# A two-layer encoder trunk on one core: where three pieces of work stand in the written order, and how the input is cut

## The chip, the cores and the metric

The kernel runs on one core of one Trainium2 chip. The core has five engines: PE (TensorE, matrix products and transposes into the accumulation memory, PSUM), DVE (VectorE), ACT (ScalarE), POOL (GpSimd) and SP (SyncE, which here only issues DMAs). The metric is the device time of one launch in microseconds (us), as the median of several runs. A profile is one execution taken by the hardware profiler, and its span runs from the first instruction of the program to the last.

## The reference, cut to what matters

The input is `x`, 512 tokens by 1024 features in float32. Two layers follow one another.

```python
def swiglu_ffn(h, w_up, w_down):
    a, b = jnp.split(h @ w_up, 2, axis=-1)
    return (jax.nn.silu(a) * b) @ w_down

for l in range(DEPTH):                       # DEPTH = 2
    x = x + 0.5 * swiglu_ffn(rmsnorm(x, ffn1_norm[l]), ffn1_w_up[l], ffn1_w_down[l])
    x = x + mixer(rmsnorm(x, mix_norm[l]), ...)
    x = x + 0.5 * swiglu_ffn(rmsnorm(x, ffn2_norm[l]), ffn2_w_up[l], ffn2_w_down[l])
    x = rmsnorm(x, final_norm[l])
```

The mixer projects its input once (`w_in`). From the columns it computes dilated sliding-window attention in three groups of eight heads (dilations 1, 4, 16; scores, a mask, a softmax, a product with the values), a convolution of width 31 over the tokens with a layer norm and a projection, two gates, and a last projection (`w_out`).

## The kernel before

Activations lie transposed: eight tiles `xs[k]` of 128 features by 512 tokens. Every float32 product is made as three products of a high and a low part (`mm3`, L156 to L159: high by high, low by high, high by low), so each activation and each weight is kept as a pair `hi`, `lo`. A weight block is staged by `stage` (L140): one DMA of 512 KB into `raw`, a copy to `hi` on ACT (L152), a difference to `lo` on DVE (L153).

**The start** (L76 to L81, L714 to L731). Four DMAs load `xnat`, one for each 128 tokens, all 1024 features wide. For each feature block k, PE transposes a square of each of the four tiles into `ps_x` (L721). Then `gained` makes `xgh` on ACT (L174) and `xgl` on DVE (L175), with which the first feed-forward product starts. ACT also squares each `xnat` tile for the norm (L727).

**The feed-forward** `ffn` (L315). For a pair of hidden blocks m it computes the two halves of the up-projection, `ps_a` and `ps_b`, 16 groups of three matmuls of 128x512 each; then `t2` takes `ps_a` times the norm factor R (L340, DVE), a Silu (L341, ACT), the product with `ps_b` (L345, DVE) and a split (`hh`, `hl`). From m = 4 (`M7`) on, the second half goes through `proj7`, which saves products by a seven-product scheme (84 matmuls of 128x256). It needs sums of the activations: `sums7` (L265), for each of four pairs of feature blocks: two additions into `t2` (L324), then L269 to L271, and a split (`Th`, `Tl`). These sums are written ahead of the loop over m. `deferred` (L349) is, in the second layer's first feed-forward, the rescaling of `xs` by the last layer's final norm: eight DVE instructions (L780) that read `R1`. It is written behind m = 0. R and R1 reach all partitions by two products each on PE (`ps_bc`, L214), which end the preceding feed-forward.

**The attention** `attend` (L507). It is called for three groups and two halves of the heads. A unit is one block of 128 queries in group 0 (four units for a call) and two blocks in the others (two units). It computes scores into two PSUM tiles `ps_S` (L528), one for each parity e of the head. For each e in turn it then does: a mask with a row minimum on DVE into `sp` (L541), exponentials on ACT (L547), four transposes on PE into `ps_T` (L550), and a copy on ACT into `PT` (L552). Then come sixteen products with the values into `ps_pv` (L558). Around the units lie the projections of the next group (`ps_n`, evicted by L451 and L483, transposed by L473), and on DVE the 480 convolution taps (L620), written behind them all.

**What sets the order.** The order on each engine is fixed when the program is built. A planner plays the program through and gives each engine, whenever it is free, the ready instruction that is written earliest; the staging of weights and a few other parts are moved up. On the chip each engine then works its list strictly in that order. A tile name has a fixed number of buffers, which its tiles share: `t2` has 2 buffers for the sums and the hidden blocks together, `sp` and `PT` share 6, `raw` has 2, `hi` and `lo` have 4 each. Of the eight PSUM banks `ps_a` and `ps_n` use 3, all of `ps_b`, the four of `proj7`, `ps_x`, `ps_S`, `ps_T`, `ps_pv` and `ps_qT` share 4 (tag "at"), and `ps_bc` uses the one that is left. A new feed-forward takes its memory over from the one before it once all readers of that are done.

```python
t2 = fp.tile([P, 2, S], F32, tag="t2", name=uniq("g2"), bufs=2)    # L322, sums
t2 = fp.tile([P, 2, S], F32, tag="t2", name=uniq("t2"), bufs=2)    # L337, hidden block
sp = slot("sp", 6)                                                 # L531
t = slot("sp", 6, name="PT")                                       # L551
```

Of the kernel before, what the change touches and what calls it, by code (L numbers as in the profile page):

```python
# [11 lines left out]
F32 = mybir.dt.float32  # L12
F32R = mybir.dt.float32r
AF = mybir.ActivationFunctionType
ALU = mybir.AluOpType
# [4 lines left out]
P = 128  # L20
D = 1024
# [23 lines left out]
def trunk(ctx: ExitStack, tc: tile.TileContext, A: dict, out: bass.AP):  # L45
# [14 lines left out]
    def ps_at(name):  # L60
        return psp.tile([P, S], F32, tag="at", name=name, bufs=4)
# [11 lines left out]

    x0s = ExitStack()
    x0 = x0s.enter_context(tc.tile_pool(name="x0", bufs=1))
    xnat = []  # L76
# [59 lines left out]
    def uniq(s):  # L136
        cnt[0] += 1
        return f"{s}_{cnt[0]}"
# [176 lines left out]
    def ffn(l, w_up, w_down, xg, R, after, deferred=None):  # L315
        wu = w_up[l].rearrange("(k p) n -> p k n", p=P)
        wd = w_down[l].rearrange("(k p) n -> p k n", p=P)
        with tc.tile_pool(name=uniq("ffn"), bufs=4) as fp:
            few.add(id(fp))
            x7 = []  # L320
            for q in range(0, KD, 2):
                t2 = fp.tile([P, 2, S], F32, tag="t2", name=uniq("g2"), bufs=2)  # L322
                for j in range(2):
                    nc.vector.tensor_add(t2[:, j], xg[q + j][0].bitcast(F32), xg[q + j][1].bitcast(F32))  # L324
                x7.append(sums7(fp, t2, xg[q:q + 2], "T", 8))
            for m0, m1 in PARTS:
                h = []
                for m in range(m0, m1, 2):
                    pss = {}
                    for ab in ((0, 1) if m < M7 else (1, 0)):  # L330
                        if ab == 1 and m >= M7:
                            o = proj7(fp, wu, FF + m * P, x7, False)
                            pss[1] = [o[:, 0], o[:, 1]]
                            continue
                        pss[ab] = [ps_mm(uniq("ps_a")) if ab == 0 else ps_at(uniq("ps_b")) for _ in range(2)]
                        proj_cols(wu, ab * FF + m * P, xg, KD, pss[ab])
# [24 lines left out]
                for ts in ((0, 1), (2, 3), (4, 5), (6,), (7,)) if last else ((0, 1), (2, 3), (4, 5), (6, 7)):  # L361
                    pss = [(ps_at if ts[0] in (0, 4, 7) else ps_mm)(uniq("ps_d")) for _ in ts]
                    proj_cols(wm, ts[0] * P, h, m1 - m0, pss)
                    for k, ps in zip(ts, pss):
                        take(k, ps, 0.5)


    def mixer(l, xg, R, rr, after):
# [5 lines left out]
        with ExitStack() as mx:  # L374
            mp = mx.enter_context(tc.tile_pool(name=uniq("mix"), bufs=2))

            def slot(tag, bufs, dt=F32, name=None):
                return mp.tile([P, S], dt, tag=tag, name=uniq(name or tag), bufs=bufs)
# [128 lines left out]
            def attend(g, hh, qkT, V):  # L507
# [6 lines left out]
                for b2 in range(0, 4, 2):  # L514
                    po = ps_at(uniq("ps_pv"))
                    pv = po.rearrange("p (i b q) -> p i b q", i=2, b=2)
                    for bs in ([[b2], [b2 + 1]] if g == 0 else [[b2, b2 + 1]]):
                        lo, hi = 0, n
                        if g == 0:
                            lo, hi = (64 if bs[0] == 0 else 0), (192 if bs[0] == 3 else 256)  # L520

                        pS = [ps_at(uniq("ps_S")) for _ in range(2)]
                        work = [(b, i) for b in bs for i in range(2)]
                        for w, (b, i) in enumerate(work):
                            k0 = b * P - 64 if g == 0 else b * P
                            for e in range(2):
                                hp = slice(e * 64, e * 64 + 64)
                                nc.tensor.matmul(pS[e][:, w * n + lo:w * n + hi], qkT[hp, i, b * P:(b + 1) * P], qkT[hp, 2 + i, k0 + lo:k0 + hi], start=True, stop=True)  # L528
                        PT = []
                        for e in range(2):  # L530
                            sp = slot("sp", 6)  # L531
                            sv = sp.rearrange("p (w k) -> p w k", k=n)
                            if lo:
                                nc.vector.memset(sv[:, :, :lo], 0.0)
                            if hi < n:
                                nc.vector.memset(sv[:, :, hi:], 0.0)

                            for w, (b, i) in enumerate(work):
                                c = slice(w * n + lo, w * n + hi)
                                h = 2 * i + e  # L540
                                nc.vector.tensor_tensor_reduce(  # L541
                                    out=sp[:, c], in0=pS[e][:, c], in1=mask[:, lo:hi], scale=1.0, scalar=3e38,
                                    op0=ALU.add, op1=ALU.min, accum_out=st[:, b, h:h + 1])
                            for w, (b, i) in enumerate(work):
                                c = slice(w * n + lo, w * n + hi)
                                h = 2 * i + e
                                nc.scalar.activation(sp[:, c], sp[:, c], AF.Exp, bias=st[:, b, h:h + 1], scale=-1.0, accum_out=st[:, b, UH + h:UH + h + 1])  # L547
                            pT = ps_at(uniq("ps_T"))
                            for i in range(4):
                                nc.tensor.transpose(pT[:, i * P:(i + 1) * P], sp[:, i * P:(i + 1) * P], ident)  # L550
                            t = slot("sp", 6, name="PT")  # L551
                            nc.scalar.activation(t, pT, AF.Copy)  # L552
                            PT.append(t)
                        for w, (b, i) in enumerate(work):
                            for j in range(nj):
                                for e in range(2):
                                    h = 2 * i + e
                                    nc.tensor.matmul(pv[e * 64:(e + 1) * 64, i, b - b2, :], V[b + j][:, (hh * UH + h) * HD:(hh * UH + h + 1) * HD], PT[e][:, (nj * w + j) * P:(nj * w + j + 1) * P], start=j == 0, stop=j == nj - 1)  # L558
                    for i in range(2):
                        dst = ot[i].rearrange("p (a r) -> p r a", r=dil)  # L560
                        if g == 0:
                            dst = dst[:, :, b2 * P:(b2 + 2) * P]
                        else:
                            dst = dst[:, b2 * dil // 4:(b2 + 2) * dil // 4, :]
                        nc.scalar.activation(dst, po[:, i * 256:(i + 1) * 256].rearrange("p (r a) -> p r a", a=dst.shape[2]), AF.Copy)
                for i in range(2):
                    nc.gpsimd.dma_start(od[g, 2 * hh + i], ot[i])
                so = sd[:, g, hh, :]
# [289 lines left out]
```

## Time and profile before

| what | value |
|---|---|
| median of 3 runs | 2653.77 us (2652.79 to 2654.54) |
| profiled execution | 2655.37 us |
| its span | 2653.3 us |
| PE busy | 2593.0 us, 98% |
| PE weight loads busy | 2168.9 us, 82% |
| DVE busy | 1984.0 us, 75% |
| ACT busy | 1100.8 us, 41% |
| PE on the chain that ended last | 92% |
| mean DMA rate | 101 GB/s |

A line of the profile names an engine, the line of the kernel, the operation, the tile written and the tiles read. Where an engine was idle before an instruction, the page names what ended that idle time. PEclk is the share of TensorE's full clock (2.4 GHz) that was granted: 1.00 is full speed, 0.50 is 1.2 GHz. Since PE is busy for 98% of the span, the time can fall only by what PE spends idle and by what it spends at the lower clock.

### The profile page before, as it was taken

The page shows a single profiled execution, that of the slowest core. Times are in us where ns is not written, and L with a number is a line of the kernel's source. Part 1 is how long each engine was busy: PE and PEld are TensorE (multiplying, and loading weights), DVE is VectorE, ACT ScalarE, POOL GpSimd, SP SyncE. Part 2 cuts the span into 40 slices and gives each one's busy share as a digit, 9 for nine tenths or more (in the row PEclk, how much of TensorE's full clock was granted, in tenths as well). Part 3 has the DMA queues.
Part 4 walks back from the last instruction along what each step waited for, and adds up shares of the span by engine and source line. Part 5 has one row for each costly group of instructions (what it writes and reads, how often), then busy time and mean ns, then how long its engine had stood idle before and what let it go on. Part 6 is the DMA issues. An engine that isn't in the chain of part 4 may idle for free.

```text
span 2653.3 us, 34486 instructions
## 1 busy us (share of the span) xinstructions
PE 2593.0 (98%) x13421; PEld 2168.9 (82%) x13421; DVE 1984.0 (75%) x3218; ACT 1100.8 (41%) x1651; POOL 110.8 (4%) x208
## 2 busy tenths in 40 slices
PE   8999999998999999999979999999999999999998
PEld 6888988776877788888868989887767777888887
DVE  6666669999986667666766766699999866666665
ACT  5333342243587234233433333422445773433334
POOL 1000000011011000000000000000011110000000
PEclk9999999999999999999989999999999999999999
DMA  4323333232333333232313333332323343233322
GB/s 143 104 92 108 92 108 105 84 119 89 108 108 113 111 96 104 88 111 91 101 55 111 96 104 96 103 105 88 110 88 120 104 129 104 88 104 96 108 92 80
DMA packets 245603, 268.87 MB, mean 101 GB/s; under 512 B 11624, under 2 KB 230128, under 8 KB 245440
## 3 DMA queue, kind: packets, MB, share of 16 engines
q1 hardware_dynamic: 233920, 234.91, 28.5%
q0 software_dynamic: 11504, 31.76, 4.1%
q8 instruction: 105, 1.72, 0.3%
q14 instruction: 58, 0.48, 0.1%
q10 hardware_dynamic: 16, 0.00, 0.0%
HBM read 251.75 MB, written 14.88 MB: 100 GB/s over the span
## 4 chain that ended last, share of the span: by engine, by line
PE 92%; DVE 6%; ACT 1%; issue 1%; DMA 0%; SPq 0%; ACTq 0%
PE ps_a L158 6%; PE ps_a L159 6%; PE ps_a L157 6%; PE ps_d L158 6%; PE ps_d L157 6%; PE ps_d L159 6%; PE ps L159 5%; PE ps L158 5%; PE ps L157 5%; PE ps_n L158 4%; PE ps_n L157 4%; PE ps_n L159 4%; DVE cv L620 2%; PE ps_S L528 1%; PE ps_pv L558 1%; PE ps_cp L158 1%
## 5 line engine op out<-in xcount | busy, mean ns | idle before, releaser
L152 ACT ACTIVATE hi<-raw 128x1024 fp32r<-128x1024 f32 (+1 forms) x376 | 391.5, 1042 | 698.1 <-PE ps_d L158 156.1
L153 DVE TENSOR_TENSOR lo<-raw,hi 128x1024 fp32r<-128x1024 f32 (+1 forms) x376 | 451.1, 1200 | 252.0 <-ACT hi L152 251.1
L620 DVE SCALAR_TENSOR_TENSOR cv<-u,cwc,cv 128x497 f32<-128x497 f32 (+14 forms) x480 | 335.8, 738 | 0.0
L157 PE MATMUL ps_a<-xgh,hi 128*128 128x512 f32 x704 | 275.7, 392 | 18.5 <-DVE t L340 16.2
L158 PE MATMUL ps_a<-xgl,hi 128*128 128x512 f32 x704 | 276.7, 393 | 0.6 <-DVE xgl L175 0.6
L159 PE MATMUL ps_a<-xgh,lo 128*128 128x512 f32 x704 | 276.2, 392 | 0.0
L158 PE MATMUL ps_d<-hl,hi 128*128 128x512 f32 x704 | 272.6, 389 | 0.0
L159 PE MATMUL ps_d<-hh,lo 128*128 128x512 f32 x704 | 272.6, 389 | 0.0
L157 PE MATMUL ps_d<-hh,hi 128*128 128x512 f32 x704 | 270.6, 389 | 0.0
L158 PE MATMUL ps_n<-lo,xgh 128*128 128x512 f32 x576 | 229.2, 398 | 4.2 <-DVE lo L153 4.2
L159 PE MATMUL ps_n<-hi,xgl 128*128 128x512 f32 x576 | 226.0, 393 | 0.0
L157 PE MATMUL ps_n<-hi,xgh 128*128 128x512 f32 x576 | 215.6, 396 | 4.6 <-DVE tmp L483 4.2
L157 PEld LDWEIGHTS ps_a<-xgh,hi 128*128 128x128 f32 x704 | 133.2, 189 | 46.2 <-DVE t L340 16.6
L158 PE MATMUL ps<-Tl,hi 128*128 128x256 f32 x576 | 163.0, 283 | 0.0
L159 PE MATMUL ps<-Th,lo 128*128 128x256 f32 x576 | 163.0, 283 | 0.0
L157 PE MATMUL ps<-Th,hi 128*128 128x256 f32 x576 | 162.8, 283 | 0.0
L159 PEld LDWEIGHTS ps_a<-xgh,lo 128*128 128x128 f32 x704 | 133.1, 189 | 28.4 <-issue 0.5
L158 PEld LDWEIGHTS ps_a<-xgl,hi 128*128 128x128 f32 x704 | 133.4, 190 | 27.6 <-DVE xgl L175 1.1
L157 PEld LDWEIGHTS ps_d<-hh,hi 128*128 128x128 f32 x704 | 132.2, 188 | 27.5
L159 PEld LDWEIGHTS ps_d<-hh,lo 128*128 128x128 f32 x704 | 132.1, 188 | 27.5
L158 PEld LDWEIGHTS ps_d<-hl,hi 128*128 128x128 f32 x704 | 132.1, 188 | 27.3
L166 ACT ACTIVATE hi<-sm 128x1024 fp32r<-128x1024 f32 x72 | 76.4, 1061 | 184.7 <-DVE sm L253 76.0
(266 smaller groups left out, 5506.5 us busy)
## 6 DMA issues: line engine op xcount, KB each, us to landing
raw<-in_ffn_w_up_dram SPq DMA_DIRECT2D x176, 512.0 KB, 3.5
raw<-in_w_in_dram SPq DMA_DIRECT2D x88, 512.0 KB, 3.7
raw<-in_ffn_w_down_dram SPq DMA_DIRECT2D x76, 512.0 KB, 3.4
raw<-in_w_in_dram SPq DMA_DIRECT2D x96, 256.0 KB, 3.2
raw<-in_w_conv_proj_dram SPq DMA_DIRECT2D x16, 512.0 KB, 3.4
raw<-in_w_out_dram SPq DMA_DIRECT2D x16, 512.0 KB, 3.4
vd<-tmp POOLq DMA_DIRECT2D x24, 256.0 KB, 2.4
od<-ot POOLq DMA_DIRECT2D x24, 256.0 KB, 3.2
```

The source lines that it names most:

```text
L152: nc.scalar.activation(hi[:, :m], raw[:, :m], AF.Copy)
L153: nc.vector.tensor_sub(lo[:, :m], raw[:, :m], hi[:, :m].bitcast(F32))
L157: nc.tensor.matmul(ps, ah, bh, start=first, stop=False)
L158: nc.tensor.matmul(ps, ah, bl, start=False, stop=False)
L159: nc.tensor.matmul(ps, al, bh, start=False, stop=last)
L166: nc.scalar.activation(hi, src, AF.Copy)
L528: nc.tensor.matmul(pS[e][:, w * n + lo:w * n + hi], qkT[hp, i, b * P:(b + 1) * P], qkT[hp, 2 + i, k0 + lo:k0 + hi], start=True, stop=True)
L558: nc.tensor.matmul(pv[e * 64:(e + 1) * 64, i, b - b2, :], V[b + j][:, (hh * UH + h) * HD:(hh * UH + h + 1) * HD], PT[e][:, (nj * w + j) * ...
L620: nc.vector.scalar_tensor_tensor(a[:, t0:t1], u[k][:, t0 + d:t1 + d], cw(l, j, k), a[:, t0:t1], op0=ALU.mult, op1=ALU.add)
```

## The change

Three edits, each of which moves work or cuts it otherwise; the arithmetic stays the same.

1. The four loads of the input become one tile filled by four DMAs of 256 feature columns each, all 512 tokens deep. Each still carries 512 KB, now in runs of 1 KB instead of 4 KB.
2. In `ffn` the four `sums7` are written behind the hidden block m = 0, and `deferred` behind m = 2. This holds for all four feed-forwards.
3. In `attend` a unit is cut in two functions. `scores` holds the score products and, for both e, mask and exponentials; `values` holds for both e transposes and copy, and then the products with the values. The scores of the next unit of the same call are written ahead of the values of this one. The first unit's scores of a call have nothing before them, and the last unit's values nothing ahead.

```diff
-    for tt in range(TT):
-        t = x0.tile([P, D], F32, name=f"xnat{tt}")
-        with tc.high_priority():
-            nc.sync.dma_start(t, A["x"][0, tt * P:(tt + 1) * P, :])
-        xnat.append(t)
+    xn = x0.tile([P, TT, D], F32, name="xnat")
+    xsrc = A["x"][0].rearrange("(t p) d -> p t d", p=P)
+    with tc.high_priority():
+        for c in range(0, D, 256):
+            nc.sync.dma_start(xn[:, :, c:c + 256], xsrc[:, :, c:c + 256])
+    xnat = [xn[:, tt] for tt in range(TT)]
...
             x7 = []
-            for q in range(0, KD, 2):
-                t2 = fp.tile([P, 2, S], F32, tag="t2", name=uniq("g2"), bufs=2)
...
-                x7.append(sums7(fp, t2, xg[q:q + 2], "T", 8))
             for m0, m1 in PARTS:
...
-                    if m == 0 and deferred is not None:
+                    if m == 0:
+                        for q in range(0, KD, 2):
+                            t2 = fp.tile([P, 2, S], F32, tag="t2", name=uniq("g2"), bufs=2)
...
+                            x7.append(sums7(fp, t2, xg[q:q + 2], "T", 8))
+                    if m == 2 and deferred is not None:
                         deferred()
...
+                def scores(bs):
...
+                    pS = [ps_at(uniq("ps_S")) for _ in range(2)]
...
+                    for e in range(2):
+                        sp = slot("sp", 6)
...
+                        sps.append(sp)
+                    return work, sps
+
+                def values(work, sps, pv, b2):
+                    PT = []
+                    for e in range(2):
+                        pT = ps_at(uniq("ps_T"))
...
+                        t = slot("sp", 6, name="PT")
+                        nc.scalar.activation(t, pT, AF.Copy)
+                        PT.append(t)
...
+                units = [(b2, bs) for b2 in (0, 2) for bs in ([[b2], [b2 + 1]] if g == 0 else [[b2, b2 + 1]])]
+                ahead = scores(units[0][1])
+                po = None
+                for u_, (b2, bs) in enumerate(units):
+                    now = ahead
+                    if u_ + 1 < len(units):
+                        ahead = scores(units[u_ + 1][1])
+                    if po is None:
+                        po = ps_at(uniq("ps_pv"))
                     pv = po.rearrange("p (i b q) -> p i b q", i=2, b=2)
...
+                    values(*now, pv, b2)
```

## Rows read from the trace of the kernel before

**Rows 1.** The page: busy time of PE, share of the span, instructions.
```profile
PE 2593.0 (98%) x13421; PEld 2168.9 (82%) x13421; DVE 1984.0 (75%) x3218; ACT 1100.8 (41%) x1651; POOL 110.8 (4%) x208
```
**Rows 2.** Waits of PE, whole span: who, for whom, total us, times, longest.
```profile
PE ps_a L157 <- DVE t L340: 16.2, 1, 16.2
PE ps_pv L558 <- ACT PT L552: 7.5, 11, 0.7
PE ps_T L550 <- ACT sp L547: 5.9, 7, 1.7
PE ps_x L721 <- DMA xnat<-in_x_dram: 5.6, 1, 5.6
PE ps_a L157 <- ACT xgh L174: 2.3, 1, 2.3
PE ps_a L158 <- DVE xgl L175: 0.6, 1, 0.6
```
**Rows 3.** Everything on tile xnat, last line: its four DMAs from issue to landing.
```profile
DMA to landing us min/median/max: 4.7/6.6/8.0
```
**Rows 4.** Timeline of the start: start, us, engine, line, op, tiles, count, [idle before].
```profile
1.23 1.92 SPq L80 DMA_DIRECT2D xnat<-in_x_dram  x4
9.29 3.54 PE L721 MATMUL ps_x<-ident,xnat 128*128 128x128 f32 x16 [5.64 <-DMA xnat<-in_x_dram]
12.41 1.04 ACT L727 ACTIVATE sqn<-xnat 128x1024 f32<-128x1024 f32 x1
14.39 2.39 ACT L174 ACTIVATE xgh<-ps_x,gcol 128x512 fp32r<-128x512 f32 x4
15.12 0.73 PE L157 MATMUL ps_a<-xgh,hi 128*128 128x512 f32 x2 [2.28 <-ACT xgh L174]
```
**Rows 5.** Timeline of the second layer's first feed-forward, DVE and PE.
```profile
1356.09 2.50 DVE L324 TENSOR_TENSOR g<-xgh,xgl 128x512 f32<-128x512 f32 x4 [9.19 <-PE ps_bc L214]
1377.68 0.75 DVE L271 SCALAR_TENSOR_TENSOR ts<-ts,g 128x256 f32<-128x256 f32 x2
1378.36 1.88 DVE L340 TENSOR_TENSOR t<-ps_a,R 128x512 f32<-128x512 f32 x3
1379.09 0.79 PE L157 MATMUL ps_a<-xgh,hi 128*128 128x512 f32 x1 [16.22 <-DVE t L340]
1383.25 1.28 DVE L345 TENSOR_TENSOR t<-ps_b,t 128x512 f32<-128x512 f32 x2
1387.31 0.28 PE L157 MATMUL ps<-xgh,hi 128*128 128x256 f32 x1
1397.38 0.40 PE L157 MATMUL ps_a<-xgh,hi 128*128 128x512 f32 x1
1397.62 0.40 PE L158 MATMUL ps_a<-xgl,hi 128*128 128x512 f32 x1
```
**Rows 6.** DVE by line, 1356 to 1388: busy us, mean ns, idle before.
```profile
L780 DVE SCALAR_TENSOR_TENSOR x<-x,pcol,ps_bc 128x512 f32<-128x512 f32 x8 | 5.4, 742 | 0.0
```
**Rows 7.** Stretches: length, busy us and count of PE, PEld, DVE, ACT, POOL; PEclk; DMA.
```profile
1356.10:1385.40 29.30, 13.08 (x46) 10.24 (x45) 28.63 (x47) 10.41 (x12) 0.00 (x0) 0.71 0.06 18
545.00:640.00 95.00, 93.78 (x475) 72.92 (x475) 92.96 (x194) 36.34 (x83) 6.74 (x12) 1.00 0.34 104
650.00:665.00 15.00, 12.15 (x58) 8.94 (x58) 15.00 (x33) 7.59 (x18) 1.30 (x2) 0.54 0.08 20
1975.00:1986.00 11.00, 9.51 (x47) 7.49 (x46) 10.99 (x27) 6.87 (x16) 1.30 (x2) 0.53 0.10 25
750.00:850.00 100.00, 99.60 (x533) 77.99 (x533) 67.75 (x165) 90.98 (x166) 12.62 (x23) 1.00 0.32 99
```
**Rows 8.** Timeline of attention units of group 0, first layer, ACT and DVE.
```profile
641.78 0.60 ACT L552 ACTIVATE PT<-ps_T 128x512 f32<-128x512 f32 x1 [1.70 <-PE ps_T L550]
641.87 0.42 DVE L541 CUSTOM_DVE_ANT_0 sp<-ps_S,mask 128x256 f32<-128x256 f32 x1
```
**Rows 9.** ACT by line, 740 to 850, the exponential's table loads: busy us, mean ns, idle.
```profile
L547 ACT ACT_TABLE_LOAD x7 | 9.0, 1283 | 0.4 <-DVE st L541 0.3
```

More of the change, by code (lines that the diff above doesn't have):

```diff
@@ L320, in ffn @@
             x7 = []
-            for q in range(0, KD, 2):
-                t2 = fp.tile([P, 2, S], F32, tag="t2", name=uniq("g2"), bufs=2)
-                for j in range(2):
-                    nc.vector.tensor_add(t2[:, j], xg[q + j][0].bitcast(F32), xg[q + j][1].bitcast(F32))
-                x7.append(sums7(fp, t2, xg[q:q + 2], "T", 8))
             for m0, m1 in PARTS:
@@ L348, in ffn @@
                         h.append(tuple(x[:, j] for x in h2))
-                    if m == 0 and deferred is not None:
+                    if m == 0:
+                        for q in range(0, KD, 2):
+                            t2 = fp.tile([P, 2, S], F32, tag="t2", name=uniq("g2"), bufs=2)
+                            for j in range(2):
+                                nc.vector.tensor_add(t2[:, j], xg[q + j][0].bitcast(F32), xg[q + j][1].bitcast(F32))
+                            x7.append(sums7(fp, t2, xg[q:q + 2], "T", 8))
+                    if m == 2 and deferred is not None:
                         deferred()
@@ L513, in attend @@
                 ot = [slot("ot", 4) for _ in range(2)]
-                for b2 in range(0, 4, 2):
-                    po = ps_at(uniq("ps_pv"))
-                    pv = po.rearrange("p (i b q) -> p i b q", i=2, b=2)
[L517 to L558, printed above, removed]
@@ new lines, in scores @@
+                def scores(bs):
+                    lo, hi = 0, n
+                    if g == 0:
+                        lo, hi = (64 if bs[0] == 0 else 0), (192 if bs[0] == 3 else 256)
+                    pS = [ps_at(uniq("ps_S")) for _ in range(2)]
+                    work = [(b, i) for b in bs for i in range(2)]
+                    for w, (b, i) in enumerate(work):
+                        k0 = b * P - 64 if g == 0 else b * P
+                        for e in range(2):
+                            hp = slice(e * 64, e * 64 + 64)
+                            nc.tensor.matmul(pS[e][:, w * n + lo:w * n + hi], qkT[hp, i, b * P:(b + 1) * P], qkT[hp, 2 + i, k0 + lo:k0 + hi], start=True, stop=True)
+                    sps = []
+                    for e in range(2):
+                        sp = slot("sp", 6)
+                        sv = sp.rearrange("p (w k) -> p w k", k=n)
+                        if lo:
+                            nc.vector.memset(sv[:, :, :lo], 0.0)
+                        if hi < n:
+                            nc.vector.memset(sv[:, :, hi:], 0.0)
+                        for w, (b, i) in enumerate(work):
+                            c = slice(w * n + lo, w * n + hi)
+                            h = 2 * i + e
+                            nc.vector.tensor_tensor_reduce(
+                                out=sp[:, c], in0=pS[e][:, c], in1=mask[:, lo:hi], scale=1.0, scalar=3e38,
+                                op0=ALU.add, op1=ALU.min, accum_out=st[:, b, h:h + 1])
+                        for w, (b, i) in enumerate(work):
+                            c = slice(w * n + lo, w * n + hi)
+                            h = 2 * i + e
+                            nc.scalar.activation(sp[:, c], sp[:, c], AF.Exp, bias=st[:, b, h:h + 1], scale=-1.0, accum_out=st[:, b, UH + h:UH + h + 1])
+                        sps.append(sp)
+                    return work, sps
@@ new lines, in values @@
+                def values(work, sps, pv, b2):
+                    PT = []
+                    for e in range(2):
+                        pT = ps_at(uniq("ps_T"))
+                        for i in range(4):
+                            nc.tensor.transpose(pT[:, i * P:(i + 1) * P], sps[e][:, i * P:(i + 1) * P], ident)
+                        t = slot("sp", 6, name="PT")
+                        nc.scalar.activation(t, pT, AF.Copy)
+                        PT.append(t)
+                    for w, (b, i) in enumerate(work):
+                        for j in range(nj):
+                            for e in range(2):
+                                h = 2 * i + e
+                                nc.tensor.matmul(pv[e * 64:(e + 1) * 64, i, b - b2, :], V[b + j][:, (hh * UH + h) * HD:(hh * UH + h + 1) * HD], PT[e][:, (nj * w + j) * P:(nj * w + j + 1) * P], start=j == 0, stop=j == nj - 1)
@@ new lines, in attend @@
+                units = [(b2, bs) for b2 in (0, 2) for bs in ([[b2], [b2 + 1]] if g == 0 else [[b2, b2 + 1]])]
[7 more added lines that the diff above has]
+                        po = ps_at(uniq("ps_pv"))
+                    pv = po.rearrange("p (i b q) -> p i b q", i=2, b=2)
+                    values(*now, pv, b2)
+                    if bs[-1] != b2 + 1:
+                        continue
@@ L565, in attend @@
                         nc.scalar.activation(dst, po[:, i * 256:(i + 1) * 256].rearrange("p (r a) -> p r a", a=dst.shape[2]), AF.Copy)
+                    po = None
                 for i in range(2):
```

1 line of the change is left out of this document (removed).

## The prediction

> **What bounds the kernel now.** The page comes first: PE is busy 2593.0 of 2653.3 us [rows 1], so 60 us of idle time, and whatever PE works at the lower clock, is all that reordering can win. The second view, PE's waits, says where the idle time is [rows 2]: one stall of 16.2 us in a feed-forward, 13.4 us in many short waits for the attention's copies and exponentials (7.5 + 5.9), and 8.5 us at the start for the input and its first split (5.6 + 2.3 + 0.6). Each of the three edits is aimed at one of these; the rest (the first identity tile, DVE late with weight splits, the tail) no edit touches. Timelines of the three places [rows 3 to 6, 8] show what released PE; stretches with the granted clock [rows 7] show what the lower clock adds.
>
> **The input in column pieces.** The four DMAs are issued from 1.23 to 3.15 us and land 4.7 to 8.0 us after issue [rows 3, 4], so the first is there at about 5.9 us and the last at about 10.7. PE needs all four now for the first block, and begins at 9.29; 16 transposes take until 12.83. Then it waits 2.28 us, because ACT squares the `xnat` tiles first, the last of them at 12.41, and makes `xgh` only at 14.39 [rows 4]. With columns, one piece gives two whole blocks, and squaring has to wait for all pieces, so that `xgh` comes ahead of it on ACT. That takes the 2.28 us away, and the 0.61 us for `xgl` behind it [rows 2], 2.9 in all, if the piece with block 0 is ready where PE starts now. Best case: it lands first, at 5.9; four transposes (a quarter of 3.54, 0.9) and one `xgh` (0.6) give a first product at 7.4 instead of 15.12, so a gain of up to 7 us. Worst case: it lands last, at 10.7, with all 16 transposes behind it: 14.2, a gain of 0.9. PE now starts well after the first landing, so the landing order isn't the order in which PE needs the tiles, and I see no reason why it should be with pieces: I take 3, and 0.9 to 7 as ends. The bytes are the same, and the 512 KB weight blocks already move in 1 KB runs. The issues stay at four on SP, nothing new stands behind them.
>
> **The sums behind m = 0, the rescaling behind m = 2.** In the second layer's first feed-forward the chain is: the new memory is free at 1356.09 (the second `ps_bc` is done), DVE then makes the sums and the rescaling, and the first eviction of `ps_a` (L340) comes at 1378.36, right behind the last L271 of the sums at 1377.68 [rows 5]. This fits buffers handed out in written order: `t2` has two, and four sums stand ahead of m = 0. PE ran out of banks at 1362.87 and stood 16.22 us. Written behind m = 0, its eviction can begin at 1356.1, and PE has a bank long before 1362.9. What is late next? PE continues with the last 24 matmuls of m = 2 (8.2 us now, 1379.09 to 1387.31, part of it at the lower clock; at 0.24 each, as from 1397.38 to 1397.62 [rows 5], 5.8), until 1368.7, and then comes to `proj7` for m = 4. Its third and fourth products need the banks of m = 2's `ps_b`, and so m = 2's own eviction, whose `t2` now stands behind all four sums. DVE is the limit there: busy 28.63 of the 29.3 us from 1356.1 to 1385.4 [rows 7], and m = 2's first L345 ended at 1384.5 [rows 5]. Of that only the rescaling leaves (L780, eight, 5.4 us [rows 6]); the order of the rest doesn't shorten it. So that L345 ends at about 1384.5 - 5.4 = 1379.1. By then `proj7` has done 12 of 84 matmuls; the other 72 take 72/84 of 10.07 us (1387.31 to 1397.38), 8.6, to 1387.7, against 1397.4 now: 9.7 us won. A new idle stretch of about 9 us lies in it, so the lower clock after it is likely paid as now (8.2 - 5.8 = 2.4): I take 8, near the lower of 9.7 and 7.3. Ends: 4, if the planner puts sums and weight splits still further ahead, and 18.6, the whole stall and its slow matmuls, if m = 2 is evicted between the sums. Costing nothing: the rescaling later, since `xs` is next needed by the down-projection many tens of us on, and the same move in the other three feed-forwards, where PE doesn't wait at this place now; if that cover were gone, it would cost at most m = 0's own eviction each, six instructions like those of [rows 5], some 4 us.
>
> **Attention.** Inside a unit the two halves run one after the other: the copy `PT` of one half starts at 641.78 and the mask of the other at 641.87 [rows 8]. `sp` and `PT` share one set of buffers, and in written order the second half's `sp` stands behind the first half's `PT`. So a unit is a chain of two masks, two exponentials, two transposes and two copies, each waiting for the other engine, and DVE puts taps between. While PE has projections of the next group this costs nothing: 545 to 640 us, PE busy 93.78 of 95 [rows 7]. Behind 640 us, and at the like place of the second layer, that filler has run out; as I read the code, its `z` buffers wait for transposes that stand behind the last unit. There PE idles, most of the 13.4 us [rows 2], and the clock falls: 0.54 over 15 us and 0.53 over 11 us [rows 7] means half clock for 13.8 and 10.3 us, in which PE was busy for about 11.2 and 8.9 (12.15/15 and 9.51/11 of them); at full clock that work takes half as long, so 5.6 + 4.4 = 10.0 us are lost. Price of the whole place: 23.4 us. With the change both masks of a unit follow each other, and those of the next unit run during transposes and products. Units pass faster, so filler returns sooner and lasts. But one unit in four of a group-0 call, its last, has nothing written ahead: I take three quarters, 17.5 us, between 0 and 23.4. Number and length of instructions stay. DVE, full there, does the same work; its taps end at the same time, and the convolution's result is needed far later.
>
> **The sum.** 3 + 8 + 17.5 = 28.5 us off the profiled execution's 2655.4 gives 2626.9. It lies 1.6 above the median of the runs, so the median falls from 2653.8 to 2625.
>
> **Rivals.** All times are medians, counted from 2653.8. (a) The clock stays low: if the units still run without projections between them, the waits shrink to a quarter, but the 10 us at half clock stay: 3 + 8 + 10 gives 2633. For it: from 650 to 665 us the clock stays low although PE has work for 12.15 of 15 us [rows 7]. Against it: quicker units bring the filler back. (b) The sums don't hold up `proj7`, and the feed-forward gives 18.6: 3 + 18.6 + 17.5 is 39, 2615. (c) The attention's waits only move, since PE is held by its four "at" banks, which two units now share: only 3 + 8 remain, 2643. (d) Slower: the second transposes of a unit need a bank that only the next unit's first mask frees; PE's list is strict, so each tap ahead of that mask now stops PE, filler or not. Today's 18 waits average 0.74 us [rows 2]; 64 halves (32 units) at 0.74 are 47 us, 34 more than now, which with 3 + 8 gives 2677. It decides once more than about 33 of the 64 halves wait ((13.4 + 11)/0.74). Against it: masks are written ahead of taps, and the next unit's scores lie a whole unit earlier. (e) ACT becomes the bound beside the gates: from 750 to 850 us it is busy 90.98 of 100 us [rows 7], since exponentials and the gates' sigmoids alternate there, with a table load of 1.28 us at each turn [rows 9]. Exponentials that come earlier can fall between other sigmoids; from 8 more loads in such a stretch on (9.0/1.28 = 7) PE would wait. There are 7 loads for exponentials now [rows 9], and as many back; 14 more are 18 us, 9 over the reserve, 18 in both layers: 2625 + 18 is 2643. Against it: two units' exponentials side by side make fewer turns, not more. The Trainium skill, "ScalarE: Activation LUTs", section "Table sets: the hidden batching unit", asks for just this, all calls of one table set before the next, which speaks against exponentials written ahead into the gates' stretch. It counts about 2.66 us for a switch with its drain; by that (14 times 2.66, less 9, twice: 56), (e) would stand at an estimated 2681. The trace shows 1.28 and work right behind it, so the trace's price is used. That the edits do nothing is unlikely: each changes the written order at a stall whose releaser is named.
>
> **How the numbers follow.** Forecast 0.49 (2625, own range 2615 to 2632), (a) 0.17, (b) 0.11, (c) 0.12, (d) 0.05, (e) 0.03, nothing at all 0.03. The low end, 2608, lies between (b) with the input's early end, 2611, and all three edits in full (7 + 18.6 + 23.4 = 49), 2605; the high end is (c). Between them lie the forecast and (a), (b), (c), (e), 0.92 less their tails. A measurement of this kernel tells 0.2%, 5.3 us, from no change. Nothing is within it, (d) is slower by more, the others faster by more: faster 0.92, same 0.03, slower 0.05.
>
> **What would show it.** Right: the first product before 13 us; no wait for `t` at L340 over 16 us, but one of 8 to 10 us at the first `proj7` of that feed-forward; both masks of a unit side by side, and PE's waits for `sp` and `PT` below 5 us in sum, with no half clock at 640 to 665. Wrong: PE's waits for `ps_T` or `ps_S` banks spread over all units, or a first product still at 15 us.

## The result, and the profile after

The changed kernel takes 2611.7 us (median of four runs, 2610.6 to 2612.8) where the kernel before, run beside it, takes 2654.0: a ratio of 0.9841, with a 95% interval of 0.9828 to 0.9853. The forecast was 2625, its range 2608 to 2643: the time is in the range, 13 us below the forecast, and below the forecast's own range of 2615 to 2632. The profiled execution took 2611.35 us, its span is 2609.6. All medians here and below are of executions at the usual clock: one of edit 3 alone, at a granted clock of 0.848 (2848 us), is left out.

The page's busy times, after; [rows 1] is the same line of before.

```profile
PE 2574.2 (99%) x13421; PEld 2161.0 (83%) x13421; DVE 1983.0 (76%) x3218; ACT 1076.7 (41%) x1634; POOL 110.2 (4%) x208
```

The span is 43.7 us shorter. PE's idle time fell from 60.3 to 35.4 us, so 24.9 of the 43.7 are idle time; the other 18.8 are busy time, with the same 13421 instructions. Where they went is read from the start of the same work on PE in both traces (tile views; us from the span's start):

| PE starts | before | after | shift |
|---|---|---|---|
| first product, `ps_a` | 15.12 | 10.87 | -4.2 |
| first mixer, `ps_gg` | 373.2 | 369.5 | -3.7 |
| its last projection, `ps_o` | 923.6 | 899.5 | -24.1 |
| second layer's first down-projection, `ps_d` | 1429.3 | 1401.6 | -27.7 |
| second mixer's last projection, `ps_o` | 2241.5 | 2198.2 | -43.3 |
| end of the span | 2653.3 | 2609.6 | -43.7 |

So the start gave 3.7 us, the two mixers 20.4 and 15.7, that one feed-forward 3.6. The other stages are as long as before.

**The start** (timeline of after; compare [rows 4]).

```profile
0.74 0.99 SPq L151 DMA_DIRECT2D raw<-in_ffn_w_up_dram  x2
1.78 2.75 SPq L80 DMA_DIRECT2D xnat<-in_x_dram  x4
7.73 3.38 PE L740 MATMUL ps_x<-ident,xnat 128*128 128x128 f32 x16 [4.08 <-DMA xnat<-in_x_dram]
8.88 0.69 ACT L174 ACTIVATE xgh<-ps_x,gcol 128x512 fp32r<-128x512 f32 x1 [1.91 <-PE ps_x L740]
10.87 0.71 PE L157 MATMUL ps_a<-xgh,hi 128*128 128x512 f32 x2
12.58 1.06 ACT L746 ACTIVATE sqn<-xnat 128x1024 f32<-128x1024 f32 x1
```

`xgh` now stands ahead of the squares on ACT, and PE begins 5.95 us after the first issue of a piece. The pieces landed 5.9 to 8.9 us after their issue here, and PE waited for the earliest. The first issue itself is later than before (1.78 us, before 1.23): two weight blocks now stand ahead of the input in the DMA list of SP, where before it was one. With edit 2 alone they stand so too, and the first issue is at 1.78.

**The mixers.** The same work of the first mixer and of the second as one stretch each, before (length, busy us and count of PE, PEld, DVE, ACT, POOL; PEclk; DMA):

```profile
462.00:902.00 440.00, 427.92 (x2155) 334.92 (x2154) 383.21 (x780) 222.61 (x440) 46.46 (x85) 0.98 0.35 106
1784.70:2219.90 435.20, 423.05 (x2154) 332.06 (x2153) 382.89 (x780) 221.22 (x439) 46.45 (x85) 0.98 0.35 107
```

and after:

```profile
458.40:877.90 419.50, 415.37 (x2154) 329.64 (x2153) 381.87 (x779) 209.64 (x431) 46.15 (x85) 1.00 0.36 111
1757.10:2176.60 419.50, 414.13 (x2154) 328.28 (x2153) 381.63 (x779) 209.68 (x431) 46.16 (x85) 1.00 0.36 111
```

Both mixers now take the same 419.5 us. PE's idle time in them falls from 12.1 + 12.2 to 4.1 + 5.4, so by 14.7 us; its busy time falls by 12.6 + 8.9 = 21.5. Part of that is the clock. The stretches at half clock inside the two mixers were, before:

```profile
650.87:664.52 13.65, 10.80 (x49) 7.87 (x46) 13.65 (x31) 7.31 (x16) 1.30 (x2) 0.50 0.09 22
865.91:869.32 3.41, 3.41 (x10) 2.67 (x9) 2.02 (x4) 0.63 (x1) 1.08 (x2) 0.50 0.87 253
1852.36:1855.77 3.41, 3.41 (x10) 2.65 (x9) 3.11 (x7) 1.06 (x1) 2.07 (x4) 0.50 0.47 179
1975.24:1985.48 10.24, 8.75 (x41) 6.90 (x40) 10.23 (x26) 6.35 (x15) 1.30 (x2) 0.50 0.10 27
```

and after:

```profile
505.61:509.03 3.42, 3.42 (x9) 2.63 (x8) 3.42 (x6) 0.28 (x1) 0.00 (x0) 0.50 0.75 180
```

PE was busy at half clock for 26.4 us in them before and for 3.4 after. At full clock that work takes at best half as long, so the clock gives back at most 11.5 of the 21.5 us.

What PE does between the units shows in the stretch of tile `ps_n` alone (busy us of PE, PEld, DVE). Before, at the place of [rows 8]:

```profile
640.00:662.00 22.00, 0.09 (x1) 0.00 (x0) 0.74 (x1) 0.75 0.15 38
```

After, at the like units:

```profile
598.00:620.00 22.00, 16.14 (x64) 11.19 (x62) 0.73 (x1) 1.00 0.37 109
```

Before, 22 us of units hold no projection; now 64 products of `ps_n` lie among them, and PE is never idle. No wait of PE for `sp` or `PT` is left in the whole span; the four masks of a unit follow one another (for example, one unit's at 605.9, 606.2, 606.5 and 606.7).

**The feed-forward** (timeline of DVE and PE after; compare [rows 5]).

```profile
1332.00 0.69 DVE L251 TENSOR_TENSOR sm<-raw 128x512 f32<-128x512 f32 x1 [9.19 <-PE ps_bc L214]
1332.61 1.28 DVE L335 TENSOR_TENSOR t<-ps_a,R 128x512 f32<-128x512 f32 x2
1335.61 3.38 DVE L799 SCALAR_TENSOR_TENSOR x<-x,pcol,ps_bc 128x512 f32<-128x512 f32 x5
1339.24 2.06 DVE L799 SCALAR_TENSOR_TENSOR x<-x,pcol,ps_bc 128x512 f32<-128x512 f32 x3
1342.35 0.69 DVE L340 TENSOR_TENSOR t<-ps_b,t 128x512 f32<-128x512 f32 x1
1347.27 0.39 PE L157 MATMUL ps<-xgh,hi 128*128 128x256 f32 x1 [1.62 <-ACT hi L166]
1357.66 1.29 DVE L335 TENSOR_TENSOR t<-ps_a,R 128x512 f32<-128x512 f32 x2
1360.13 0.58 PE L158 MATMUL ps<-Tl,hi 128*128 128x256 f32 x1 [1.99 <-DVE Tl L167]
1361.72 1.29 DVE L340 TENSOR_TENSOR t<-ps_b,t 128x512 f32<-128x512 f32 x2
```

The eviction of m = 0 (now L335) comes 0.6 us behind the memory's release, and the stall of 16.2 us is gone. PE's waits of after, those at `proj7` of this feed-forward (tile `ps`), sum to 9.6 us:

```profile
PE ps L157 <- ACT Th L166: 2.9, 2, 1.5
PE ps L158 <- DVE Tl L167: 2.6, 2, 2.0
PE ps L159 <- DVE lo L167: 2.0, 1, 2.0
PE ps L157 <- ACT hi L166: 1.6, 1, 1.6
...
PE ps L157 <- ACT s L302: 0.5, 1, 0.5
```

The same work, from the first `ps_b` to the first `ps_d`, as one stretch before:

```profile
1329.10:1429.30 100.20, 83.98 (x442) 71.85 (x441) 67.92 (x104) 34.93 (x42) 0.00 (x0) 0.91 0.25 79
```

and after:

```profile
1305.00:1401.60 96.60, 87.03 (x441) 73.93 (x440) 67.91 (x104) 35.05 (x41) 0.00 (x0) 0.91 0.27 82
```

Idle time falls by 16.22 - 9.57 = 6.65 us, busy time rises by 3.05: the clock is at half speed for as long as before (17.06 us, from 1348.7 now, from 1367.7 before), but PE is busy for 10.0 us of it, where before it was busy for 5.6 and the half speed lay mostly over the stall.

### The profile page after: what moved, and what is told of

The parts are those of the page before. It is cut to its first block, busy times and chain, and to the rows that moved or that the text cites. A ratio compares the mean times of both kernels' runs of the same rounds, so it can differ in the third digit from the quotient of the medians.

```text
span 2609.6 us, 34504 instructions
## 1 busy us (share of the span) xinstructions
PE 2574.2 (99%) x13421; PEld 2161.0 (83%) x13421; DVE 1983.0 (76%) x3218; ACT 1076.7 (41%) x1634; POOL 110.2 (4%) x208
## 4 chain that ended last, share of the span: by engine, by line
PE 94%; DVE 4%; ACT 1%; issue 0%; DMA 0%; SPq 0%; DVEq 0%; ACTq 0%
PE ps_d L157 6%; PE ps_d L158 6%; PE ps_d L159 6%; PE ps_a L158 6%; PE ps_a L157 6%; PE ps_a L159 6%; PE ps L158 5%; PE ps L159 5%; PE ps_n L157 5%; PE ps L157 5%; PE ps_n L158 5%; PE ps_n L159 4%; PE ps_S L526 2%; PE ps_pv L562 2%; PE ps_T L554 1%; PE ps_cp L159 1%
## 5 line engine op out<-in xcount | busy, mean ns | idle before, releaser
L166 ACT ACTIVATE hi<-raw 128x1024 fp32r<-128x1024 f32 x72 | 76.4, 1061 | 196.8 <-PE ps_d L158 69.4
```

The source lines that it names most:

```text
L166: nc.scalar.activation(hi, src, AF.Copy)
```

## The experiments

The theory behind the prediction was that two pairs of steps share buffers handed out in written order (`sp` with `PT`, sums with hidden blocks), and that this order, not the work, makes engines wait. The rivals: the written order of the steps decides by itself; the clock decides; the parts help only together. All medians stand beside the kernel before of the same series, 2653.8 to 2654.5.

**One edit at a time.** Edit 3 alone:

> The kernel before with edit 3 alone (attention cut in scores and values, the next unit's scores written ahead). Theory: the three edits add up, and the attention alone carries what the comparison of the two traces puts in the two mixers, 20.4 and 15.7 us: 36 us less than before, about 2618. Rival: part of the mixers' gain comes from the earlier start of the work ahead of them (another phase of weights, taps and units); then this edit alone gives what was forecast for it, about 17.5 us, 2636.

Measured 2618.15 us, ratio 0.9865 (0.9848 to 0.9881): 36 us. The attention carries five sixths of the result without the other two edits.

Edit 1 alone:

> The kernel before with edit 1 alone (the input in four pieces of 256 columns). Theory: the shift of 3.7 us that the changed kernel shows from the first feed-forward on is all from here and is kept to the end: 2650.1. Rival: with the attention as before, the earlier start is given back at the attention's waits or at DVE's taps, and under 1 us is left, 2653.

Measured 2657.8, ratio 1.0013 (1.0004 to 1.0023): a few us slower. Yet at the start it gains more than in the changed kernel: one weight block stands ahead of the input, the first issue is at 1.24, the first transposes begin at 6.02, 4.8 us after it, and the first product at 9.35.

```profile
6.02 3.68 PE L721 MATMUL ps_x<-ident,xnat 128*128 128x128 f32 x16 [2.36 <-DMA xnat<-in_x_dram]
...
9.35 1.17 PE L157 MATMUL ps_a<-xgh,hi 128*128 128x512 f32 x2
```

The lead is 5.5 us at the first mixer and 8.6 at the second; in the second mixer 9.2 us are lost. Its stretch:

```profile
1776.00:2220.40 444.40, 429.05 (x2155) 334.77 (x2154) 383.05 (x781) 226.34 (x443) 46.30 (x85) 0.97 0.34 105
```

PE's waits, whole span:

```profile
PE ps_T L550 <- ACT sp L547: 12.6, 9, 2.9
PE ps_pv L558 <- ACT PT L552: 7.5, 11, 0.7
```

444.4 us against 435.2, with PE's waits for `sp` at 12.6 us against 5.9 [rows 2]. In the order in which DVE runs them, the instructions of the two programs differ in the first 54 us, then not until 646 us, in the middle of the first mixer, and behind that some 300 of 3218 stand elsewhere: with another start the planner laid the mixers out anew, and the chain of halves came out worse. So the lead was won and lost again. The rival's end (nothing left) held, for more than the reason it gave. The profiled executions differ by only 0.6 us (2655.99 and 2655.37), so the trace accounts for the lost lead and not for all of the 3.3 us by which the medians differ.

Edit 2 alone:

> The kernel before with edit 2 alone (sums behind m = 0, rescaling written behind m = 2). Theory: the 16 us stall goes, and most of it comes back as waits of proj7, as in the changed kernel, where this feed-forward came out 3.5 us shorter: 2651. Rival 1: the forecast's 8 us, 2646. Rival 2: as with the input, the planner lays out the second layer's attention anew behind it, in its old form, and that moves the time by up to 9 us either way, whatever the feed-forward gives.

Measured 2656.18, ratio 1.0007 (0.9997 to 1.0016): no difference that can be told. The feed-forward gains 4.1 us (shift from -1.9 to -6.0), with the same waits at `proj7` as in the changed kernel; the second mixer loses 7.3, with 9.2 us of waits for `sp`. Rival 2 held.

So the three edits don't add up. Alone they come to 36.4, -3.3 and -2.4 us, 30.7 in sum, where together they give 42.3. Edits 1 and 2 are worth about 6 us together beside edit 3, and each nothing alone.

**The buffers of the attention.** Nothing is moved, only the names of buffers:

```diff
-                            sp = slot("sp", 6)
+                            sp = slot("sp", 3)
...
-                            t = slot("sp", 6, name="PT")
+                            t = slot("PT", 3)
```

> The kernel before with one difference: the attention's copies PT have three buffers of their own, and sp three, in place of six that both share; the written order stays, nothing is looked ahead. Theory (the prediction's): the second half's mask waits for the first half's PT because the buffers are handed out in written order; with buffers of their own the two halves of a unit can run side by side, and half or more of the 36 us goes, so 2617 to 2636. Rival 1: what costs is the written order itself (the planner gives each engine the earliest written work, and a whole unit must lie ahead); then under 6 us go, 2648 to 2654. Rival 2: three buffers of a kind hold the units closer together than six did, and it is slower than before, by up to 10 us.

Measured 2620.7, ratio 0.9873 (0.9858 to 0.9888): 33.8 us, nearly all that edit 3 gives, with the old written order and no more memory. What is left of the waits in the units:

```profile
PE ps_T L550 <- ACT sp L547: 1.3, 1, 1.3
PE ps_pv L558 <- ACT PT L552: 0.2, 1, 0.2
```

From 598 to 620 us, 72 products of `ps_n` lie between the units. The order of masks and copies shows what the names changed. In group 0 of both layers the second half's first mask starts ahead of the first half's copy in 3 of 16 units before, and in 15 of 16 here (one unit's masks start at 612.7, 613.0, 613.4 and 613.7, its copies at 621.5 and 622.1). The shared buffers are the cause.

Both halves together, nothing written ahead (the diff is against edit 3 alone):

```diff
-                ahead = scores(units[0][1])
...
-                    now = ahead
-                    if u_ + 1 < len(units):
-                        ahead = scores(units[u_ + 1][1])
+                    now = scores(bs)
```

> The kernel before with edit 3 without its looking ahead: a unit's scores, both masks and both sets of exponentials are written together, then both transposes, copies and the products; the next unit starts behind them. Theory: the chain of two halves is half of the evil, the missing work ahead the other half: about 18 us less than before, 2636. Rival 1: looking ahead is all that counts (PE has nothing else between scores and transposes): under 6 us, 2648 to 2654. Rival 2: it counts for nothing, since both halves together already give PE enough: 30 us or more, 2624 or less.

Measured 2626.06, ratio 0.9897 (0.988 to 0.9913): 28 us. Taking the first `PT` from between the two masks is four fifths of edit 3; looking a unit ahead adds about 8 us. Both theory (18) and rival 1 fell; it is near rival 2.

The changed kernel with own buffers too, `sp` 4 and `PT` 2:

> The changed kernel with buffers of their own for sp (4) and PT (2) in place of six for both. Theory: with the scores written ahead both masks of a unit already stand ahead of its copies, so that the shared order holds nothing any more: within 3 us of the changed kernel, 2609 to 2614. Rival 1: the shared order still costs at the units' ends: 5 us or more less, 2606. Rival 2: two buffers for PT hold the products back: 5 us or more over it, 2617.

Measured 2608.26, ratio 0.9827 (0.9812 to 0.9842): about 3 us under the changed kernel, between theory and rival 1. The two intervals overlap, but the traces agree: from the first `ps_n` to the first `ps_o` the mixers are 2.7 and 1.8 us shorter. So the shared order most likely still costs a little.

Own buffers (as in the first of these) with edit 1:

> The kernel before with own buffers for sp (3) and PT (3) and, besides, the input in column pieces. Theory: the input's 4 to 6 us were lost only in the attention's chain of halves; with that chain gone they are kept: 4 to 6 us less than with own buffers alone (2620.7), 2615 to 2617. Rival: whatever starts earlier is laid out anew and ends by chance; 2619 to 2624.

Measured 2619.52, ratio 0.987 (0.9853 to 0.9886), 1.2 us under own buffers alone. In the profile the lead is 6.7 us at the first mixer, 4.7 at the first of its gates (`ps_gc`), 7.6 at the second (`ps_gA`), and 3.2 from its last projections to the end. So part is kept, most is not, and neither text is borne out: what a lead of some us is worth at the end isn't settled by the chain of halves alone.

**The feed-forward.** The sums get a buffer of their own, in the kernel before and at their old place:

```diff
-                t2 = fp.tile([P, 2, S], F32, tag="t2", name=uniq("g2"), bufs=2)
+                t2 = fp.tile([P, 2, S], F32, tag="g2", name=uniq("g2"), bufs=1)
...
-        w = pool.tile([P, 4, HT], F32, tag="w4", name=uniq("ts"), bufs=3)
+        w = pool.tile([P, 4, HT], F32, tag="w4", name=uniq("ts"), bufs=2)
...
-        o = pool.tile([P, 4, HT], F32, tag="w4", name=uniq("o7"), bufs=3)
+        o = pool.tile([P, 4, HT], F32, tag="w4", name=uniq("o7"), bufs=2)
```

> The kernel before with a buffer of their own for the sums (one pair of 128x512, beside the two of the hidden blocks; for the room, the second buffers of the seven-product scheme, w4, go from three to two). The sums stay written ahead of the loop. Theory: the 16.2 us stall for the eviction comes from the two t2 buffers handed out in written order, as the attention's chain came from sp and PT; with a buffer of their own the eviction (L340) can start right behind the memory's release and the wait for it falls from 16.2 to under 7 us (rescaling and first sums still ahead), without moving a line. What comes back at proj7 is about 10 us, as in the runs with the sums moved. Whole time: 2645 to 2658, as the second layer's attention is laid out anew. Rival: the planner prefers the sums because they are written first; then the stall stays at 14 us or more.

Measured 2649.56, ratio 0.9982 (0.9972 to 0.9991). The eviction follows the release (DVE):

```profile
1355.18 1.29 DVE L324 TENSOR_TENSOR g<-xgh,xgl 128x512 f32<-128x512 f32 x2 [9.19 <-PE ps_bc L214]
1356.99 1.28 DVE L340 TENSOR_TENSOR t<-ps_a,R 128x512 f32<-128x512 f32 x2
```

No wait of PE for it is left; 8.9 us come back at `proj7`, and this feed-forward is 5.0 us shorter. Here too the order of buffers, not that of the lines, held the eviction back.

The rescaling left out of the changed kernel:

> The changed kernel without the rescaling of xs by the final norm of the first layer: its eight DVE instructions are left out, and with them that part of the result. Theory: in the changed kernel these 5.4 us still run ahead of m = 0's products and of the sums, and are what is late at proj7; without them PE's waits there (9.6 us) shrink by about 5.4 us and the lower clock behind them is shorter: 5 to 8 us less than the changed kernel, 2604 to 2606. Rival: DVE's sums and weight splits hold proj7 by themselves, so that only 0 to 2 us go, 2610 or more.

Measured 2606.42, ratio 0.982 (0.9805 to 0.9835): 5 us under the changed kernel; the waits at `proj7` are 6.2 us, and the feed-forward is 6.5 us shorter: 3.4 us of idle time and 3.1 of busy time, as the half clock lasts 6.8 us instead of 17.1. The eight instructions cost what the theory says, though the waits shrink by less than their 5.4 us.

R1's broadcast moved into the rescaling, so that it can't run early:

```diff
-                    R1 = broadcast_psum(r1, pool)
-                    def rescale(l=l):
+                    def rescale(pool, l=l, r1=r1):
+                        R1 = broadcast_psum(r1, pool)
```

> The changed kernel with the broadcast of R1 (four small DVE products and one product on PE) moved from the end of the feed-forward before into the rescaling itself, so that both come behind m = 2 on PE, and the old memory is free one broadcast earlier. Theory: DVE begins some 5.5 us earlier than at 1332.0 and has the 5.4 us of rescaling out of the way; PE's waits at proj7 (9.6 us) go nearly all, and with them the stretch at half clock behind them (17.07 us, in which some 6 to 8 us are lost): 10 to 16 us less than the changed kernel, 2596 to 2602. Rival 1: only the waits get smaller and the clock falls all the same: 5 us, 2606. Rival 2: the broadcast's product, now in the middle of m = 2's, waits for its DVE part and stops PE; no gain, 2611.

Measured 2609.13, ratio 0.9831 (0.9816 to 0.9845). DVE began at 1326.91, but the rescaling fell into the middle of the sums:

```profile
1344.42 0.42 DVE L270 SCALAR_TENSOR_TENSOR ts<-ts,g 128x256 f32<-128x256 f32 x1
1345.03 0.75 DVE L799 SCALAR_TENSOR_TENSOR x<-x,pcol,ps_bc 128x512 f32<-128x512 f32 x1 [0.20 <-PE ps_bc L214]
1346.83 2.72 DVE L799 SCALAR_TENSOR_TENSOR x<-x,pcol,ps_bc 128x512 f32<-128x512 f32 x4
1349.80 2.06 DVE L799 SCALAR_TENSOR_TENSOR x<-x,pcol,ps_bc 128x512 f32<-128x512 f32 x3
```

and `proj7` then waited 4.7 us for one `Th` made of those sums, 7.2 us in all. The feed-forward is 4.6 us shorter, and the second mixer 3.8 longer (423.3 for 419.5 us). Neither the theory's size nor rival 2. The theory counted 6 to 8 us lost in the stretch at half clock; PE was busy for 10.0 us of it in the changed kernel, so at most 5 could be won there.

The rescaling taken from DVE (ACT the gain, POOL the factor):

```diff
-                            nc.vector.scalar_tensor_tensor(xs[kk], xs[kk], pc("final_norm", l, kk), R1, op0=ALU.mult, op1=ALU.mult)
+                            nc.scalar.activation(xs[kk], xs[kk], AF.Copy, scale=pc("final_norm", l, kk))
+                            nc.gpsimd.tensor_mul(xs[kk], xs[kk], R1)
```

> The changed kernel with R1's broadcast moved into the rescaling (as in the run before) and the rescaling taken from DVE: ACT multiplies by the gain, POOL by a copy of R1. Theory: DVE begins some 5 us earlier and has nothing of the rescaling between the sums; PE's waits at proj7, 9.6 us in the changed kernel, 6.2 without the rescaling and 7.2 with it late, go to 2 us or less, the half clock behind them mostly too: this feed-forward 8 to 13 us shorter than in the changed kernel; 2598 to 2604 if the later layout keeps that. Rival 1: ACT's part, written as early as the planner finds room, pushes back the splits (Th, hh) that proj7 waits for; 3 us or less. Rival 2: POOL's work slows DVE beside it; the same small gain, with longer DVE instructions there.

Measured 2608.28, ratio 0.9827 (0.9812 to 0.9842); the feed-forward is 4.4 us shorter, no more than with the rescaling on DVE. The waits at `proj7` are still 8.8 us, 6.6 of them for one `Tl` of DVE; the gain is busy time, as the half clock lasts 10.2 us. Rival 2 held. DVE by line while POOL works (1345.4 to 1358.2; busy us, mean ns), and POOL:

```profile
L348 DVE TENSOR_TENSOR g<-xgh,xgl 128x512 f32<-128x512 f32 x2 | 3.4, 1750 | 0.0
L271 DVE SCALAR_TENSOR_TENSOR ts<-ts,g 128x256 f32<-128x256 f32 x2 | 2.9, 1490 | 0.0
L335 DVE TENSOR_TENSOR t<-ps_a,R 128x512 f32<-128x512 f32 x2 | 1.3, 676 | 0.0
...
L801 POOL TENSOR_TENSOR x<-x,R 128x512 f32<-128x512 f32 x8 | 12.8, 1627 | 489.9 <-ACT R L798 489.9
```

The same with own buffers for `sp` (4) and `PT` (2):

> The kernel with the rescaling on ACT and POOL and R1 late, and besides buffers of their own for sp (4) and PT (2). Theory: the two add up, the buffers gave 3 us: 2595 to 2602. Rival: the attention's layout moves the time by some us either way and hides what the buffers gave: 2602 to 2609.

Measured 2604.63, ratio 0.9811 (0.9797 to 0.9826): under both kernels, about 7 us under the changed one (0.9841). The two gains, about 3 us each and each hardly clear of its interval, added up.

## Why the prediction was right, and where not

The total lay in the range partly by luck: of the three terms two fell outside their own ends, one low and one high, and the figure nearest to the measured time is that of a rival which fell, (b) with 2615.

**Input, 3 us forecast, 3.7 measured.** The 2.28 us behind the squares went as said. The reason given for 3 rather than 7, that the landing order isn't the order of need, fell: in two traces PE began 4.8 and 5.95 us after the first issue, which are the shortest landings (4.7 and 5.9). Two things kept the best case, a first product at 7.4, away (15.12 less 7.4 is 7.7, which the working puts as 7). The first piece, issued behind two weight blocks, landed at 7.7 and not at 5.9; that is 1.8 us, and comes with edit 2. And all 16 transposes of four blocks still stand ahead of the first product on PE (7.73 to 11.1), where the working let four do: 3.1 us from the first transpose to the first product instead of 1.5. So the 3 us came out near for another reason than the one given. That this lead lasts was taken for granted, and it holds only beside edit 3: alone it was lost in the second mixer.

**Feed-forward, 8 forecast, 3.6 measured, below the lower end of 4.** The cause of the stall held (own buffer for the sums), and so did its return at `proj7`: 9.6 us, forecast about 9. Two steps failed. First, "of that only the rescaling leaves": it didn't leave. It is written behind m = 2, but the planner takes whatever is ready, and put all eight between m = 0's first factor and its product (1335.61 to 1341.3, product at 1342.35). Without them 5 us more go, and m = 2's product begins at 1356.5. The wait also had another shape: not one for m = 2's eviction, but seven short ones for sums and weight splits, and m = 2's product began at 1361.72, where by the working it would have ended at 1355 (1379.1 less the 24.1 of the shift). Second, the clock: "likely paid as now", 2.4 us. The low stretch is as long as before, but broken waits put it over work (10.0 us of it, before 5.6): busy time is 3.05 us longer than before, and half of the 4.4 us more at half clock, 2.2, is most of that.

**Attention, 17.5 forecast, 36 measured, above the upper end of 23.4.** The mechanism, buffers handed out in written order, is shown by the run that changes the buffers alone. The size failed twice. The factor of three quarters was wrong: the last unit of a call needs nothing ahead, since the halves side by side do four fifths of the work, and projections then fill the rest. And the price of the place was too low: 36.2 us went, where 23.4 were counted. Idle time fell by 14.7 us, near the 13.4 of [rows 2]. The clock gave back at most 11.5, near the 10.0 counted. What is left, 10 us or more, was counted as nothing: it is busy time of PE at full clock. The prediction's first step, that idle time and the lower clock are all that reordering can win, was wrong by that much, and so is the like sentence under the profile before.

Where these 10 us lie shows in the short products. Two kinds in the first mixer by form (busy us, mean ns of one), before, from 664.6 to 865.8 us, all at full clock:

```profile
L528 PE MATMUL ps_S<-qkT 64*128 64x128 f32 x128 | 15.5, 294 | 0.0
L550 PE MATMUL ps_T<-ident,sp 128*128 128x128 f32 x64 | 13.8, 284 | 0.0
```

and after, in the whole mixer:

```profile
L554 PE MATMUL ps_T<-ident,sp 128*128 128x128 f32 x128 | 22.2, 277 | 0.0
L526 PE MATMUL ps_S<-qkT 64*128 64x128 f32 x128 | 11.9, 283 | 0.0
```

One product takes nearly as long as before, but a group of them covers less time: 216 ns for each `ps_T` before and 174 after, 121 and 93 for each `ps_S`. So products overlap more than before, as fits short products that stood alone between waits and now have others beside them. Groups overlap one another and the ends of matmuls are modelled in the profile, and no run separates this from the rest, so the cause of these 10 us is argued, not shown.

**The rivals.** (a) fell: PEclk is 1.00 from 598 to 620 us. (b) fell, since the sums do hold `proj7` (9.6 us of waits). (c) and (d) fell: no wait for `ps_T` or `ps_S` is among PE's. (e) fell the other way: loads of ACT's tables went from 53 to 36, those for exponentials from 14 to 4, and ACT is busy 67.1 us from 740 to 840, where before it was 91 in the like stretch, 750 to 850 [rows 7]. The Trainium skill, "ScalarE: Activation LUTs", section "Table sets: the hidden batching unit", asks for calls of one set side by side; the trace agrees that this edit brought them together, at 1.28 us a load.

## What to carry to other kernels

When two engines hand one another a chain step by step, look first whether the steps of that chain share buffers: separate names gave 34 us here without a line moved. Writing a step later doesn't make it run later where a planner takes what is ready; only something that it needs does. A lead of some us won early is worth only what the stages behind it keep, so time each edit with and without the others, and look for the place where the shift is lost. An engine that is busy for 98% of the span can still be given time back at full clock: 10 us or more of PE's busy time went here without an instruction less.

## What the runs showed of the hardware

While POOL worked on its 128x512 products, the DVE instructions with two operands in SBUF that began behind a POOL product took about 1.07 us longer each, whatever their length: 128x512 sums 1750 ns for 689 in the changed kernel, 128x256 ones 1490 for 423. One that had begun ahead of POOL's first product was no longer than without (1226 for 1222). The eviction that reads PSUM and SBUF was not slowed (676 for 690). The Trainium skill, "SBUF — State Buffer", section "SBUF: two separate sides", says that a DVE instruction with two SBUF inputs and a GpSimd one that reads SBUF exclude one another for a whole instruction; the trace agrees.

Column pieces with runs of 1 KB landed as fast as token pieces with runs of 4 KB where one weight block was issued ahead of them: 4.7 to 7.9 us after issue with edit 1 alone, 4.7 to 8.0 before [rows 3]. Behind two weight blocks both kinds landed later: token pieces 5.5 to 8.1 us after issue with edit 2 alone, column pieces 5.9 to 8.9 in the changed kernel, and at the latest, in one of its variants, 7.2 to 10.4.
